# A change of phase in written order: the norms' rows, the next phase's first weight split, and four modulation blocks

## The chip, the cores and the metric

The kernel runs on one core of a Trainium2 chip. The metric is the device time of one execution in microseconds (us), lower is better. Below, TensorE (PE) multiplies, VectorE (DVE) and ScalarE (ACT) prepare operands, SyncE (SP) issues the DMAs.

## The reference, cut to what matters

One encoder layer over 256 tokens of 2048 channels, in fp32: half-step SwiGLU FFN, token mixing (a Conformer convolution on half of the channels beside differential attention), half-step SwiGLU FFN. Each part is normed before and after, and shifted, scaled and gated by a modulation vector.

```python
mod = silu(c) @ w_ada + b_ada                # 9 x 2048 values: sh, sc, gt of three parts
h = modulate(rms_norm(x, g_pre0), sh1, sc1)
x = x + 0.5 * gt1 * rms_norm(swiglu(h, w_gate, w_up, w_down), g_post0)
h = modulate(rms_norm(x, g_pre1), sh2, sc2)
u = h @ w_in                                 # convolution's two halves, q, k, v
m = concat(silu(layer_norm(depthwise(a * sigmoid(g)))), diff_attention(q, k, v)) @ w_out
x = x + gt2 * rms_norm(m, g_post1)
h = modulate(rms_norm(x, g_pre2), sh3, sc3)
x = x + 0.5 * gt3 * rms_norm(swiglu(h, ...), g_post2)
```

## The kernel before

**Weights.** Each fp32 product is made of three matmuls (L272 to L274) on operands split in a high and a low part. Weights come in blocks of 1 MB: `load` issues the DMA on SP into one of four `raw` buffers, ACT casts the high part (L160, tile `hi`, three buffers), DVE subtracts to get the low part (L162, `lo`); `parts` does all three. Activations are split in the same way by `split_act` (L173 on ACT, L175 on DVE). A raw buffer comes free when its `lo` is made. SP, ACT and DVE each take their instructions in the order that the program has them.

**Modulation.** `w_ada` comes in 144 blocks of 1 MB through the same four raw buffers. For each, DVE multiplies and sums (L183), and a tiny instruction (L189 or L192) adds bias or gain. A generator `bg` yields them one by one to the loops around.

**Phases.** The 256 tokens are two tiles of 128 rows. In order: FFN1 to 774 us; the first change of phase; the convolution's projection, attention, the output projection with the convolution's norm at 1057 to 1098 us; the second change; FFN2; the end. The last two column units of a projection run tile by tile in `m_last`, so that tile 0 is done first. What happens to a unit's sum is `evac` (add L486, sum of squares L236, gate L489; L847 in the mixing). After a tile's last unit, `close` norms the tile, adds it to x (L260) and `normed` makes the next phase's normed rows (L245 on ACT, L247 on DVE). A norm's small steps are L199, L204, L207 (square root on ACT, with a table load ahead of it) and L209. `front_of` then transposes the rows (L218), modulates them (L222, L225) and splits them (L227, L228), while the first weight blocks are multiplied (L311 to L313 after the first change, L272 to L274 after the second).

**What sets the order.** A scheduler orders the instructions of each engine from priorities, unless a stretch stands in `manual_schedule`, where the written order of the named engines holds. `issue_after` gives a stretch the place behind a named instruction.

**The convolution's norm.** `normalize` (L795 to L820) ends in four activation splits, `conv_acts`. The loop over the four column units behind it issues `MIXC` modulation blocks ahead of each unit's matmuls with the output weights `wo`, a list of 1 MB blocks, two for each unit and half.

## Time and profile before

| quantity | value |
|---|---|
| three runs | 1917.48, 1912.46, 1915.33 us; median 1915.33 |
| profiled execution | 1911.84 us, its span 1910.0 us |
| mean granted clock of TensorE | 0.984 |
| busy: PE, DVE, ACT | 1836.3, 1423.6, 821.4 us |

The span is the stretch from the first to the last recorded instruction; 1.84 us of the execution's own time lie around it. The profiled execution is the shortest of the four shown.

### The profile page before, as it was taken

How to read it: one execution, taken by the hardware profiler on the slowest of the kernel's cores; microseconds unless marked ns; L12 is line 12 of the kernel's file. 1: busy time of each engine (PE TensorE's matmuls, PEld its weight loads, DVE VectorE, ACT ScalarE, POOL GpSimd, SP SyncE). 2: the span in 40 equal slices, each digit the busy share in tenths (PEclk: the TensorE clock that was granted, in tenths of full speed). 3: DMA queues.
4: the chain of work that ended last, by engine and by line, in shares of the span. 5: the costliest groups of instructions: out<-in, count | busy, mean ns of one | idle time of the engine just before them, and what ended most of it. 6: DMA issues, size and time to landing. Idle time of an engine off the chain costs nothing.

```text
span 1910.0 us, 22064 instructions
## 1 busy us (share of the span) xinstructions
PE 1836.3 (96%) x8944; PEld 1542.5 (81%) x8944; DVE 1423.6 (75%) x1594; ACT 821.4 (43%) x852; POOL 6.0 (0%) x49
## 2 busy tenths in 40 slices
PE   5999999999999999799998897999999999999997
PEld 3788888888888888699997686788888888888886
DVE  7789999788889888688998967854555555555455
ACT  4544445433433334643554454544344333343342
POOL 0000000000000000000000000000000000000000
PEclk9999999999999999899999898999999999999999
DMA  9888877989999998355444665865665666565552
GB/s 362 320 317 330 337 278 290 358 345 361 357 357 370 349 367 323 122 182 185 157 174 157 242 241 202 331 238 205 236 220 205 235 220 226 215 235 210 194 193 72
DMA packets 68934, 492.58 MB, mean 258 GB/s; under 512 B 7648, under 2 KB 7776, under 8 KB 9440
## 3 DMA queue, kind: packets, MB, share of 16 engines
q1 hardware_dynamic: 68832, 491.17, 69.0%
q8 instruction: 70, 1.15, 0.2%
q14 instruction: 32, 0.26, 0.0%
HBM read 489.05 MB, written 2.10 MB: 257 GB/s over the span
## 4 chain that ended last, share of the span: by engine, by line
PE 89%; DVE 5%; ACT 3%; DMA 2%; issue 0%; SPq 0%; DVEq 0%; ACTq 0%
PE ps L273 29%; PE ps L274 29%; PE ps L272 28%; DVE lo L162 2%; DMA raw<-in_wgu 2%; ACT hi L160 1%; DVE raw L183 1%; PE ps L413 1%; ACT tmp L236 1%; PE ps L312 0%; PE ps L311 0%; DMA raw<-in_wk 0%; PE ps L313 0%; PE ps L678 0%; PE ps L218 0%
## 5 line engine op out<-in xcount | busy, mean ns | idle before, releaser
L162 DVE TENSOR_TENSOR lo<-raw,hi 128x2048 fp32r<-128x2048 f32 x314 | 718.5, 2290 | 359.8 <-ACT hi L160 359.1
L160 ACT CAST hi<-raw 128x2048 fp32r<-128x2048 f32 x314 | 600.3, 1912 | 732.4 <-PE ps L274 362.0
L272 PE MATMUL ps<-hi,big 128*128 128x512 f32 x2256 | 879.2, 395 | 16.9 <-ACT big L227 11.3
L273 PE MATMUL ps<-lo,big 128*128 128x512 f32 x2256 | 884.0, 392 | 2.8 <-DVE lo L162 2.8
L274 PE MATMUL ps<-hi,big 128*128 128x512 f32 x2256 | 881.5, 392 | 2.0 <-DVE big L175 1.2
L272 PEld LDWEIGHTS ps<-hi,big 128*128 128x128 f32 x2256 | 426.1, 189 | 106.4 <-ACT big L227 12.7
L273 PEld LDWEIGHTS ps<-lo,big 128*128 128x128 f32 x2256 | 426.5, 189 | 92.5 <-DVE lo L162 6.2
L274 PEld LDWEIGHTS ps<-hi,big 128*128 128x128 f32 x2256 | 425.7, 189 | 92.5 <-DVE big L175 2.5
L183 DVE SCALAR_TENSOR_TENSOR raw<-raw,crow 128x2048 f32<-128x2048 f32 x144 | 327.7, 2283 | 0.6 <-DMA raw<-in_wada 0.5
L272 PE MATMUL ps<-big,hi 128*128 128x256 f32 x448 | 127.3, 284 | 0.0
L273 PE MATMUL ps<-big,hi 128*128 128x256 f32 x448 | 126.7, 283 | 0.0
L274 PE MATMUL ps<-big,lo 128*128 128x256 f32 x448 | 126.7, 283 | 0.0
L630 DVE SCALAR_TENSOR_TENSOR big<-big,par,big 128x256 f32<-128x256 f32 x240 | 100.1, 477 | 0.0
L272 PEld LDWEIGHTS ps<-big,hi 128*128 128x128 f32 x448 | 85.9, 192 | 0.3 <-issue 0.3
L273 PEld LDWEIGHTS ps<-big,hi 128*128 128x128 f32 x448 | 86.0, 192 | 0.0
L274 PEld LDWEIGHTS ps<-big,lo 128*128 128x128 f32 x448 | 85.9, 192 | 0.0
L397 ACT ACTIVATE tmp<-ps 128x256 f32<-128x256 f32 x64 | 24.3, 384 | 96.3 <-PE ps L274 96.3
L486 DVE TENSOR_TENSOR big<-ps,big 128x512 f32<-128x512 f32 x48 | 32.9, 691 | 31.7 <-PE ps L274 31.7
L358 DVE TENSOR_TENSOR big<-ps,big 128x512 f32<-128x512 f32 x72 | 45.2, 681 | 5.4 <-PE ps L274 5.4
L398 DVE TENSOR_TENSOR tmp<-ps,tmp 128x256 f32<-128x256 f32 x64 | 26.1, 421 | 30.9 <-ACT tmp L397 30.9
L218 PE MATMUL ps<-ident,big 128*128 128x128 f32 x96 | 19.7, 297 | 29.6 <-DVE big L247 28.7
L173 ACT CAST big<-ps 128x512 fp32r<-128x512 f32 x44 | 25.8, 585 | 38.0 <-PE ps L413 38.0
(135 smaller groups left out, 742.6 us busy)
## 6 DMA issues: line engine op xcount, KB each, us to landing
raw<-in_wada SPq DMA_DIRECT2D x144, 1024.0 KB, 6.1
raw<-in_wgu SPq DMA_DIRECT2D x116, 1024.0 KB, 5.0
raw<-in_wd SPq DMA_DIRECT2D x88, 1024.0 KB, 5.0
raw<-in_wk SPq DMA_DIRECT2D x60, 1024.0 KB, 5.5
raw<-in_wqk SPq DMA_DIRECT2D x28, 1024.0 KB, 4.8
raw<-in_wo SPq DMA_DIRECT2D x16, 1024.0 KB, 4.8
raw<-in_wv SPq DMA_DIRECT2D x8, 1024.0 KB, 4.8
raw<-in_wkc SPq DMA_DIRECT2D x4, 1024.0 KB, 5.1
```

What stands on the lines that cost most here:

```text
L160: nc.scalar.copy(hi, raw)
L162: ins = nc.vector.tensor_tensor(out=lo, in0=raw, in1=hi.bitcast(F32), op=ALU.subtract)
L173: nc.scalar.copy(hi[:, :w], v[:, :w])
L183: nc.vector.scalar_tensor_tensor(out=raw, in0=raw, scalar=1.0, in1=crow, op0=ALU.mult, op1=ALU.mult, accum_out=acc)
L272: nc.tensor.matmul(o, ah, bh, start=first, stop=False)
L273: nc.tensor.matmul(o, ah, bl, start=False, stop=False)
L274: last_mm[0] = nc.tensor.matmul(o, al, bh, start=False, stop=last)
L358: nc.vector.tensor_tensor(out=a[t], in0=b[t], in1=a[t], op=ALU.add)
L397: nc.scalar.activation(v[:, o], b[t][:, :S], AF.Silu)
L398: nc.vector.tensor_tensor(out=v[:, o], in0=b[t][:, S:], in1=v[:, o], op=ALU.mult)
L486: nc.vector.tensor_tensor(out=y[t][u], in0=b, in1=y[t][u], op=ALU.add)
L630: nc.vector.scalar_tensor_tensor(out=cot(c), in0=vps[c][:, j:j + S], scalar=w, in1=cot(c), op0=ALU.mult, op1=ALU.add)
```

## The change

1. `evac` in the FFNs writes the gated sum to a new tile and no longer over the sum that ACT squares.
2. `m_last` takes `evac` and `close` apart from the matmuls: all matmuls of both tiles first, then, in written order for DVE and ACT, tile 0's `evac` and `close`, the first weight split of the next phase (`ahead`), tile 1's. A square root `warm` stands at its start.
3. The next phase's front is made earlier, so that its first split can be handed to `m_last`; `front_of` becomes `go_on`. A block that prepares the attention's constants moves ahead of FFN1.
4. `MIXC` goes from 2 to 4. Four modulation blocks go to the convolution's projection, one for each step; four stand behind the last activation split of the convolution's norm, where two per unit had stood.

```diff
-MIXC = 2
+MIXC = 4
@@ split_act
-        nc.vector.tensor_tensor(out=lo[:, :w], in0=v[:, :w], in1=hi[:, :w].bitcast(F32),
+        conv_last[0] = nc.vector.tensor_tensor(out=lo[:, :w], in0=v[:, :w], in1=hi[:, :w].bitcast(F32),
@@ Front and MFront (there: quarters)
+        def ahead(self):
+            self.first = parts(self.w[0])
...
-                self.wh, self.wl = parts(self.w[kt // per])
+                self.wh, self.wl = (kt == 0 and self.first) or parts(self.w[kt // per])
@@ m_last
+    ordered = lambda: tc.manual_schedule(engines={mybir.EngineType.DVE, mybir.EngineType.Activation})
+
-    def m_last(units, acts, after):
+    def m_last(units, acts, evac, close_, ahead):
...
-                after(u, t, banks[u][t])
+        with ordered():
+            if ahead:
+                nc.scalar.activation(small(1, "warm"), csil[:, 0:1], AF.Sqrt, scale=0.0)
+            xn = []
+            for t in range(NT):
+                for u, _, _ in units:
+                    evac(u, t, banks[u][t])
+                xn.append(close_(t))
+                if t == 0 and ahead:
+                    ahead()
+        return xn
@@ ffn, evac
-                    nc.vector.tensor_tensor(out=y[t][u], in0=y[t][u], in1=gb[u], op=ALU.mult)
-                if end and u == 3:
-                    xn.append(close(t, y, ss, 0.5, final))
+                    yg = big()
+                    nc.vector.tensor_tensor(out=yg, in0=y[t][u], in1=gb[u], op=ALU.mult)
+                    y[t][u] = yg
@@ convolution's projection
+        if 2 <= c < 2 + MIXC:
+            next(bg, None)
@@ output projection
-        for _ in range(MIXC):
-            next(bg, None)
+        if u == 0:
+            with tc.issue_after(conv_last[0].ins):
+                for _ in range(MIXC):
+                    next(bg, None)
```

The rows below are in the order in which an engine takes them; waits are not shown. In the changed kernel line numbers are shifted: cast L160 and low part L162 stay, activation split L173 and L175 become L175 and L177, modulation block L183, L189, L192 become L185, L191, L194, square sum L236 becomes L238, root L207 becomes L209, normed rows L245 and L247 become L247 and L249, add L486 becomes L510, gate L489 becomes L514, matmuls L272 to L274 become L274 to L276.

**First place: DVE, the last unit pair of FFN1.** The L486 and L489 (L510, L514) of `big_2524` and `big_2526` (`big_2540`, `big_2542`) are the adds and gates of unit 1; the splits read weights of units 2 and 3. Before:

```order
L183 SCALAR_TENSOR_TENSOR raw_5304,acc_5306<-raw_5304,crow 128x2048
L175 TENSOR_TENSOR big_5333<-raw_5329,big_5331 128x512
L189 TENSOR_TENSOR sh<-acc_5306,par 128x1
L175 TENSOR_TENSOR big_5337<-raw_5329,big_5335 128x512
L175 TENSOR_TENSOR big_5341<-raw_5329,big_5339 128x512
L175 TENSOR_TENSOR big_5345<-raw_5329,big_5343 128x512
L486 TENSOR_TENSOR big_2524<-ps_5237,big_2524 128x512
L486 TENSOR_TENSOR big_2526<-ps_5238,big_2526 128x512
L175 TENSOR_TENSOR big_5351<-raw_5347,big_5349 128x512
L489 TENSOR_TENSOR big_2524<-big_2524,ps_5232 128x512
L175 TENSOR_TENSOR big_5355<-raw_5347,big_5353 128x512
```

Changed:

```order
L510 TENSOR_TENSOR big_2540<-ps_5255,big_2540 128x512
L510 TENSOR_TENSOR big_2542<-ps_5256,big_2542 128x512
L514 TENSOR_TENSOR big_5330<-big_2540,ps_5250 128x512
L514 TENSOR_TENSOR big_5335<-big_2542,ps_5250 128x512
L177 TENSOR_TENSOR big_5353<-raw_5349,big_5351 128x512
L177 TENSOR_TENSOR big_5357<-raw_5349,big_5355 128x512
L162 TENSOR_TENSOR lo_5391<-raw_5387,hi_5389 128x2048
L177 TENSOR_TENSOR big_5361<-raw_5349,big_5359 128x512
L162 TENSOR_TENSOR lo_5397<-raw_5393,hi_5395 128x2048
```

The splits of the first block stood ahead of unit 1's adds and gates, and now stand behind all four of them.

**Second place: ACT, then DVE, between tile 0's norm and tile 1's.** `ssx` and `x_81` belong to tile 0, `ssy_439` to tile 1; the `hi` and `lo` are the next phase's weights `wkc`. ACT before:

```order
L236 ACTIVATE tmp_5447,ssx_984_5442<-x_81 128x512
L160 CAST hi_5691<-raw_5689 128x2048
L236 ACTIVATE tmp_5450,ssx_984_5442<-x_81 128x512
L236 ACTIVATE tmp_5453,ssx_984_5442<-x_81 128x512
L236 ACTIVATE tmp_5495,ssy_439_2231<-big_2637 128x512
L160 CAST hi_5777<-raw_5775 128x2048
L207 ACTIVATE sq_990_5458<-rs_989_5455 128x1
L236 ACTIVATE tmp_5523,ssy_439_2231<-big_2743 128x512
L245 ACTIVATE big_5464<-x_81,ri_991_5460 128x512
```

ACT changed (the table load ahead of the first root of this norm is still there, six rows higher; both `warm` roots stand at the program's start):

```order
L209 ACTIVATE sq_997_5532<-rs_996_5529 128x1
L247 ACTIVATE big_5538<-x_81,ri_998_5534 128x512
L247 ACTIVATE big_5542<-x_81,ri_998_5534 128x512
L160 CAST hi_5546<-raw_5544 128x2048
L160 CAST hi_5704<-raw_5702 128x2048
L160 CAST hi_5790<-raw_5788 128x2048
L238 ACTIVATE tmp_5551,ssy_439_2247<-big_2653 128x512
L238 ACTIVATE tmp_5556,ssy_439_2247<-big_2759 128x512
L209 ACTIVATE sq_1011_5563<-rs_1010_5560 128x1
```

DVE changed, from tile 0's normed rows:

```order
L249 TENSOR_SCALAR big_5540<-x_81,ri_998_5534 128x512
L162 TENSOR_TENSOR lo_5548<-raw_5544,hi_5546 128x2048
L510 TENSOR_TENSOR big_2653<-ps_5348,big_2653 128x512
L162 TENSOR_TENSOR lo_5706<-raw_5702,hi_5704 128x2048
L514 TENSOR_TENSOR big_5553<-big_2653,ps_5337 128x512
L510 TENSOR_TENSOR big_2759<-ps_5386,big_2759 128x512
L162 TENSOR_TENSOR lo_5792<-raw_5788,hi_5790 128x2048
L514 TENSOR_TENSOR big_5558<-big_2759,ps_5342 128x512
L201 TENSOR_REDUCE rs_1010_5560<-ssy_439_2247 128x1
L206 TENSOR_SCALAR rs_1010_5560<-rs_1010_5560 128x1
L211 RECIPROCAL ri_1012_5565<-sq_1011_5563 128x1
```

Two casts stood among tile 0's squares, the third ahead of them (not shown); now all three stand behind tile 0's normed rows and ahead of tile 1's square sums, and on DVE the three low parts stand between tile 1's adds and gates. Further on DVE a modulation block (`raw_6072`) now stands in the last norm of tile 1:

```order
L262 SCALAR_TENSOR_TENSOR x_82<-big_5558,ri_1012_5565,x_82 128x512
L201 TENSOR_REDUCE rs_1018_5580<-ssx_1013_5567 128x1
L206 TENSOR_SCALAR rs_1018_5580<-rs_1018_5580 128x1
L185 SCALAR_TENSOR_TENSOR raw_6072,acc_6074<-raw_6072,crow 128x2048
L211 RECIPROCAL ri_1020_5585<-sq_1019_5583 128x1
```

**Third place: SP, then DVE, at the convolution's norm.** SP before:

```order
L153 DMA raw_8688<-in_wada 128x2048
L153 DMA raw_8693<-in_wada 128x2048
L153 DMA raw_8698<-in_wo 128x2048
L153 DMA raw_8728<-in_wo 128x2048
L153 DMA raw_8773<-in_wada 128x2048
L153 DMA raw_8778<-in_wada 128x2048
L153 DMA raw_8783<-in_wo 128x2048
L153 DMA raw_8813<-in_wo 128x2048
L153 DMA raw_8858<-in_wada 128x2048
L153 DMA raw_8863<-in_wada 128x2048
```

SP changed:

```order
L153 DMA raw_8604<-in_wo 128x2048
L153 DMA raw_8634<-in_wo 128x2048
L153 DMA raw_8721<-in_wada 128x2048
L153 DMA raw_8726<-in_wada 128x2048
L153 DMA raw_8731<-in_wada 128x2048
L153 DMA raw_8736<-in_wada 128x2048
L153 DMA raw_8741<-in_wo 128x2048
L153 DMA raw_8771<-in_wo 128x2048
L153 DMA raw_8816<-in_wo 128x2048
L153 DMA raw_8846<-in_wo 128x2048
```

DVE changed, from the last activation splits to the first `wo` splits:

```order
L177 TENSOR_TENSOR big_8672<-big_5937,big_8670 128x512
L177 TENSOR_TENSOR big_8680<-big_5938,big_8678 128x512
L177 TENSOR_TENSOR big_8688<-big_5939,big_8686 128x512
L185 SCALAR_TENSOR_TENSOR raw_8721,acc_8723<-raw_8721,crow 128x2048
L185 SCALAR_TENSOR_TENSOR raw_8726,acc_8728<-raw_8726,crow 128x2048
L194 SCALAR_TENSOR_TENSOR gs<-acc_8723,par 128x1
L191 TENSOR_TENSOR sh<-acc_8728,par 128x1
L185 SCALAR_TENSOR_TENSOR raw_8731,acc_8733<-raw_8731,crow 128x2048
L185 SCALAR_TENSOR_TENSOR raw_8736,acc_8738<-raw_8736,crow 128x2048
L194 SCALAR_TENSOR_TENSOR gs<-acc_8733,par 128x1
L191 TENSOR_TENSOR sh<-acc_8738,par 128x1
L162 TENSOR_TENSOR lo_8745<-raw_8741,hi_8743 128x2048
L162 TENSOR_TENSOR lo_8775<-raw_8771,hi_8773 128x2048
```

The blocks of `wada` went in pairs between pairs of `wo`. Now four go in a row, and the next `wo` take the buffers that these four leave.

## Rows read from the trace of the kernel before

**Rows 1.** The page, part 1: busy us, share, instructions of each engine.

```profile
PE 1836.3 (96%) x8944; PEld 1542.5 (81%) x8944; DVE 1423.6 (75%) x1594; ACT 821.4 (43%) x852; POOL 6.0 (0%) x49
```

**Rows 2.** Waits of TensorE by what released it: total us, times, longest.

```profile
PE ps L218 <- DVE big L247: 28.7, 5, 10.9
```

**Rows 3.** TensorE, first change: start, us, line, tiles, idle before, releaser.

```profile
751.98 0.47 PE L272 MATMUL ps<-big,big 128*128 128x512 f32 x1
...
780.44 0.90 PE L218 MATMUL ps<-ident,big 128*128 128x128 f32 x3 [6.35 <-DVE big L247]
...
788.14 0.79 PE L311 MATMUL ps<-big,hi 128*128 128x256 f32 x2 [0.79 <-ACT big L227]
```

**Rows 4.** VectorE from the last unit pair of FFN1 to the second tile's norm.

```profile
750.71 1.37 DVE L486 TENSOR_TENSOR big<-ps,big 128x512 f32<-128x512 f32 x2 [0.80 <-PE ps L274]
...
776.33 0.68 DVE L486 TENSOR_TENSOR big<-ps,big 128x512 f32<-128x512 f32 x1
777.03 2.29 DVE L162 TENSOR_TENSOR lo<-raw,hi 128x2048 fp32r<-128x2048 f32 x1
...
781.50 2.74 DVE L260 SCALAR_TENSOR_TENSOR x<-big,ri,x 128x512 f32<-128x512 f32 x4
...
785.90 0.88 DVE L247 TENSOR_SCALAR big<-x,ri 128x512 f32<-128x512 f32 x2
```

**Rows 5.** ScalarE at the first change.

```profile
752.58 0.62 ACT L236 ACTIVATE tmp<-big 128x512 f32<-128x512 f32 x1
...
765.68 1.28 ACT L207 ACT_TABLE_LOAD   x1
766.98 0.20 ACT L207 ACTIVATE sq<-rs 128x1 f32<-128x1 f32 x1
...
775.12 1.88 ACT L160 CAST hi<-raw 128x2048 fp32r<-128x2048 f32 x1
```

**Rows 6.** VectorE at the convolution's norm.

```profile
1084.27 1.74 DVE L813 RECIPROCAL tmp<-tmp 128x256 f32<-128x256 f32 x1
...
1088.35 3.25 DVE L818 SCALAR_TENSOR_TENSOR big<-big,par,tmp 128x256 f32<-128x256 f32 x8
1091.52 2.28 DVE L183 SCALAR_TENSOR_TENSOR raw<-raw,crow 128x2048 f32<-128x2048 f32 x1
...
1097.35 1.28 DVE L175 TENSOR_TENSOR big<-big,big 128x512 fp32r<-128x512 f32 x2
```

**Rows 7.** TensorE at the convolution's norm.

```profile
1079.62 0.67 PE L783 MATMUL ps<-tmp,onesc 128*128 128x256 f32 x2
...
1086.65 0.65 PE L131 MATMUL ps<-ident,gt 128*128 128x128 f32 x4 [1.60 <-ACT tmp L853]
1090.73 0.80 PE L272 MATMUL ps<-hi,big 128*128 128x512 f32 x1 [3.43 <-ACT big L173]
...
1094.47 1.22 PE L274 MATMUL ps<-hi,big 128*128 128x512 f32 x2 [1.24 <-DVE big L175]
```

**Rows 8.** Busy time by stretch; the column behind POOL is TensorE's granted clock.

```profile
830.00:860.00 30.00, 30.00 (x252) 30.00 (x252) 27.89 (x46) 11.62 (x9) 0.00 (x0) 1.00 0.59 213
1088.00:1098.00 10.00, 6.03 (x13) 4.31 (x14) 10.00 (x19) 5.37 (x12) 0.00 (x0) 0.50 0.66 235
```

**Rows 9.** DMA issues between 1040 and 1172 us: KB each, median us to landing.

```profile
raw<-in_wo SPq DMA_DIRECT2D x10, 1024.0 KB, 4.9
```

**Rows 10.** VectorE at the second change.

```profile
1149.44 2.29 DVE L162 TENSOR_TENSOR lo<-raw,hi 128x2048 fp32r<-128x2048 f32 x1 [1.73 <-ACT hi L160]
1151.65 0.68 DVE L847 TENSOR_TENSOR big<-ps,tmp 128x512 f32<-128x512 f32 x1
...
1158.47 2.29 DVE L162 TENSOR_TENSOR lo<-raw,hi 128x2048 fp32r<-128x2048 f32 x1 [1.53 <-ACT hi L160]
...
1160.87 0.88 DVE L247 TENSOR_SCALAR big<-x,ri 128x512 f32<-128x512 f32 x2
```

**Rows 11.** VectorE at the end of the program.

```profile
1901.92 0.69 DVE L489 TENSOR_TENSOR big<-big,ps 128x512 f32<-128x512 f32 x1 [1.13 <-ACT tmp L236]
```

More of the change, by code (lines that the diff above doesn't have):

```diff
@@ L168, in parts @@
         return hi, lo
+    conv_last = [None]
     def split_act(v, w=512):
@@ L296, in __init__ @@
             self.sum = None
+            self.first = None
+        def ahead(self):
+            self.first = parts(self.w[0])
         def step(self, kt, first, last):
@@ L335, in __init__, with ahead @@
             self.sum = None
+            self.first = None
+        def ahead(self):
+            self.first = quarters(self.w[0])
         def step(self, kt, first, last):
@@ L343, in step @@
                 if i % 4 == 0:
-                    self.parts = quarters(self.w[i // 4])
+                    self.parts = (i == 0 and self.first) or quarters(self.w[i // 4])
                 for t in range(NT):
@@ L451, in leave, with ffn @@
             left.append(f)
-    def ffn(l, h, front, facts, wgu, wd, bg, every, final):
+    def ffn(l, h, front, facts, wgu, wd, bg, every, ahead):
         y = [[None] * 4 for _ in range(NT)]
@@ L462, in tick @@
                 next(bg, None)
-        xn = []
         hacts = [(a[:, :S], a[:, S:]) for a in h]
@@ L502, in ffn @@
                     gb[u] = gate_row(l, u)
-                m_last([(u, srcs(u), None) for u in range(4 - N_LAST, 4)], acts, evac)
+                xn = m_last([(u, srcs(u), None) for u in range(4 - N_LAST, 4)], acts, evac,
+                            lambda t: close(t, y, ss, 0.5, not ahead), ahead)
         return xn
@@ L556, in first_front, with go_on @@
         return h, facts
-    def front_of(l, xn, wk, late):
-        h = []
-        front = Front(wk, h, SET[l]) if l == 1 else MFront(wk, h, SET[l] // 2)
+    def go_on(l, xn, h, front, late):
         n_late = 0
@@ L571, in front_of @@
                 front.step(i - LEAD, i == LEAD, i == NK + LEAD - 1)
-        return h, front
     xn = []
@@ L590, in block_kernel @@
     h, facts = first_front(xn, wk1, ada_of([(m, kt) for kt in range(NK) for m in (1, 0)]), bg)
-    xn = ffn(0, h, None, facts, wgu1, wd1, bg, EVERY1, False)
     lv = cp.tile([P, 4, DH], F32, tag="lv", name="lv")
@@ L612, in block_kernel @@
     nc.vector.tensor_scalar(out=nlam, in0=nlam, scalar1=-LAM_INIT, scalar2=None, op0=ALU.add)
-    h = []
+    h1 = []
+    front = Front(wkc[0], h1, SET[1])
+    xn = ffn(0, h, None, facts, wgu1, wd1, bg, EVERY1, front.ahead)
+    h = h1
     need([(m, kt) for m in (3, 4) for kt in range(NK)], bg)
-    h, front = front_of(1, xn, wkc[0], iter(()))
+    go_on(1, xn, h, front, iter(()))
     co = [big() for _ in range(NC_ // 2)]
@@ L840, in block_kernel @@
     need([(5, kt) for kt in range(NK)], bg)
-    xn = []
     gb = {}
@@ L847, in mix_evac @@
         nc.vector.tensor_tensor(out=y[t][u], in0=b, in1=gb[u], op=ALU.mult)
-        if u == 3:
-            xn.append(close(t, y, ss, 1.0, False))
     for u in range(4):
@@ L861, in block_kernel @@
                 mix_evac(u, t, open_[u][t])
-    m_last([(u, of_conv(u), open_[u]) for u in range(4 - N_LAST, 4)], conv_acts, mix_evac)
-    h, front = front_of(2, xn, wk2[0], bg)
-    ffn(2, h, front, {}, wgu2, wd2, ada_of([(8, kt) for kt in range(NK)]), 6, True)
+    h = []
+    front = MFront(wk2[0], h, SET[2] // 2)
+    xn = m_last([(u, of_conv(u), open_[u]) for u in range(4 - N_LAST, 4)], conv_acts, mix_evac,
+                lambda t: close(t, y, ss, 1.0, False), front.ahead)
+    go_on(2, xn, h, front, bg)
+    ffn(2, h, front, {}, wgu2, wd2, ada_of([(8, kt) for kt in range(NK)]), 6, None)
 def _layout(i):
```

## The prediction, made before the changed kernel was run

> **What bounds the kernel now.** I read the page first: TensorE is busy for 1836.3 of 1910.0 us, 96% [rows 1], so an edit is worth what it adds to or takes from TensorE's waits, and VectorE at 75% matters where it stands ahead of TensorE. The list of TensorE's waits comes next: the largest is the transposes L218 behind the normed rows L247, 28.7 us in five waits, the longest 10.9 [rows 2]; these are the two changes of phase and the start. The timelines then show each place. At the first change the matmuls end at 780.44 - 6.35 = 774.09, and the next phase's first matmul starts at 788.14 [rows 3], 14.05 us later. At the convolution's norm TensorE waits 1.60, 3.43 and 1.24 us, 6.27 in all, from 1085.05 on [rows 7], with the clock at half (0.50) from 1088 to 1098 [rows 8]. In the second change the last normed rows start at 1160.87 [rows 10].
>
> **The change, part by part, made against the profiled execution's 1911.84 us.** I follow the printed order of the changed kernel, with durations from the rows.
>
> *First change, the splits ahead of it.* In the changed order the casts and low parts of units 2 and 3 stand behind unit 1's adds, squares and gates. The second square of unit 1 now has no cast ahead of it, so it ends near 752.9 instead of 752.58 + 0.62 + 0.19 = 753.4 [rows 5], but the first cast (0.6) only then starts: 753.5. The matmul that started at 751.98 [rows 3] starts at 753.5, 1.5 us late; behind it TensorE waits some 0.4 for the first low part and some 0.6 for the first full cast of 1.9. 96 matmuls took 751.98 to 774.09, 0.23 each; they now end near 776.4, **+2.3**. Fifty-six of them, the last one of tile 0 among these, are done at 753.5 + 1.0 + 56 x 0.23 = 767.4.
>
> *First change, the norms.* Tile 0: add 0.7, square 0.8, table load 1.28 [rows 5], root and reciprocal 0.5, so L260 starts at 770.7; an undisturbed L260 to L247 takes 785.90 - 781.50 = 4.40 [rows 4], so the normed rows start at 775.1. ACT gives its two rows until 776.4 and then takes the three weight casts, 1.9 each [rows 5], to 782.1. VectorE has the three low parts, 2.2 us from one start to the next instruction's (2.29 with the end that overlaps) [rows 4], between tile 1's adds and gates: the first at 778.3, after the cast, then add, low part, gate, add, low part, gate, each small one 0.6. That ends at 778.3 + 3 x 2.2 + 4 x 0.6 = 787.3. What is queued there is tile 1's whole norm, and TensorE waits for that. Sum, root and reciprocal 0.8, then 4.40: 792.5. In this last norm stands a modulation block ahead of the reciprocal. Its buffer comes free with the third low part at 786.7, a block lands 4.9 us after its issue [rows 9], 791.6, and it holds VectorE for 2.2 from 791.9 on: the normed rows start at 794.4. From there to the first matmul it was 788.14 - 785.90 = 2.24 [rows 3, 4]: 796.6. That is 8.5 late, **2.3 + 6.2**. Before, one low part lay beside TensorE's own matmuls and one of them, 777.03, in the way. The bounds: 785.3 if nothing stood between (776.4 + 0.7 + 0.8 + 0.8 + 4.40 + 2.24), that is -2.8, and with a second block's wait +11.
>
> A rule says otherwise about the table load: the Trainium skill, ScalarE: Activation LUTs, section What ACT_TABLE_LOAD costs, counts 1.28 us and a drain of 1.38 for each switch of set. The row shows the load at 765.68 and the root at 766.98, 1.30 later [rows 5], with no drain; by the page tile 0's rows and all behind them would come 1.4 later and the whole sum would be 16.2 instead of 14.8. The measurement decides here.
>
> *`warm`.* Both roots stand at the program's start, so no load leaves a norm's path; 0, between -1.28 and 0 per change if they stood where they are written.
>
> *Convolution's norm.* The matmuls of the second mean (1079.62 [rows 7]) stand nine matmuls earlier, 2.1 us; with root and reciprocal (1.74 [rows 6]) the products L818, at 1088.35 before, start near 1081.2, because the modulation blocks and low parts between are gone. The last activation split, done at 1097.35 + 1.28 = 1098.6 [rows 6], is done near 1087.9 (I take ACT's part, 6.7 us behind the first product). This is 10 us early, and not what TensorE waits for next. The four modulation blocks sit in all four raw buffers, and the first `wo` block can be issued only when the first of them is through VectorE, behind the norm: 1087.9 + 2.2 = 1090.1; it lands 4.9 later [rows 9], 1095.0, is cast until 1096.9, and its low part stands behind all four blocks and their tiny sums: 1087.9 + 4 x 2.2 + 0.6 = 1097.3, plus 2.2 = 1099.5. TensorE has two matmuls without the low part (0.85 at half clock) and the gate's (0.65): from 1085.05 to 1099.5 it waits 14.45 - 1.5 = 12.95 instead of 6.27. The half clock lies in both: before it covered thirteen matmuls [rows 8], now about as many behind the resume. **+6.7**; bounds +2.5 (first block landed sooner and the low part ahead of the last two modulation blocks) and +9.
>
> *The four blocks in the projection.* 4 x 2.28 us of VectorE where TensorE is full and VectorE busy 27.89 of 30 us [rows 8]. 0: the convolution's own products are fillers that can slip; without that cover up to 9.
>
> *Second change.* Before, a low part stood ahead of tile 1's gate (1149.44 to 1151.65) and one in its last norm (1158.47) [rows 10]. Now one stands ahead of the gates and one behind the first sum, waiting for its cast; the last norm is free. I get the normed rows at 1160.2, and one split of the next phase less made beforehand, which VectorE catches up. **-1**, between -4 (nothing between) and +2.2 (the missing split lies in the way).
>
> *End.* The same lateness of the splits costs 1.2; the last gate, which waited 1.13 for the square [rows 11], no longer does, and then the square is what ends last: 0.6 back. **+0.6**. The constants' block ahead of FFN1 lies beside VectorE's free quarter: 0.
>
> Sum: 2.3 + 6.2 + 6.7 - 1.0 + 0.6 = **+14.8**, 1926.6 for the profiled execution's like. That one is the shortest of four; the mean of 1911.84, 1912.46, 1915.33 and 1917.48 is 1914.3, so I forecast 1914.3 + 14.8 = **1929**.
>
> **Rivals.** *The norm alone sets the resume.* If at all three places the weights' splits are ready whenever a norm ends, the first change gives -2.8, the norm of the convolution -6.27 and the 2.6 that thirteen matmuls lose at half clock, the second -4, the end +0.6: -15, 1899. For it: the norm's rows do become contiguous. Against: three casts stand by the printed order ahead of tile 1's first square, and the `wo` blocks have no buffer. It decides at whether tile 0's rows are done before about 768, so that three casts and low parts fit ahead of 776.4; I have 775.1.
>
> *The buffers are not in the way.* If the modulation blocks pass VectorE ahead of the norm's end, so that `wo` has landed by 1088, the convolution's norm gives -8.9 and the rest stays: 8.5 - 8.9 - 1.0 + 0.6 = -0.8, 1914, no change. Against: the printed order has all four behind the last activation split.
>
> *The blocks in the projection are not covered*: up to +9, 1938.
>
> **How the numbers follow.** The forecast has 0.70, the buffers' rival 0.14, the norm alone 0.12, the uncovered blocks 0.04. No change means within 0.3%, 5.7 us, of the median 1915.33, about what three runs can tell. The forecast's own range is 1921 to 1938 (first change 11 to 4, convolution 9 to 2.5, second change 2.2 to -4, not all at one end). To hold 8 in 10 the range reaches down to the buffers' rival: 1913 to 1938. Faster 0.12, same 0.14, slower 0.74.
>
> **What would show it.** Right: the first L311's like starts 20 us behind the last matmul of FFN1 instead of 14; on ACT three casts of 1.9 in a row ahead of tile 1's square; a VectorE low part ends the wait at the convolution's norm, near 13 us in all, with `wo` landing behind the first modulation block. Wrong: normed rows of tile 1 within 9 us of TensorE's last matmul, `wo` issued ahead of the modulation blocks, or waits in the projection, where there were none.

## The result, and the profile after

The changed kernel takes 1926.96 us (median of 1925.57 to 1927.87), the kernel before 1914.76 beside it (1912.46 to 1917.48): ratio 1.007, 95% interval 1.0054 to 1.0085. It is slower, as forecast; 1929 was 2 us too high.

The profiled execution took 1927.59 us with a span of 1925.8. The first part of its page, and TensorE's waits by what released them (total us, times, longest):

```profile
PE 1836.6 (95%) x8944; PEld 1542.2 (80%) x8944; DVE 1424.6 (74%) x1594; ACT 822.7 (43%) x855; POOL 6.0 (0%) x49
```

```profile
PE ps L220 <- DVE big L249: 34.9, 4, 18.1
PE ps L274 <- ACT hi L160: 13.5, 4, 9.3
...
PE ps L274 <- ACT big L175: 2.3, 2, 1.2
```

TensorE is busy as long as before [rows 1] to 0.3 us, so nearly the whole difference is idle time. The wait for the normed rows (L220 behind L249, which were L218 and L247) grew from 28.7 us [rows 2] to 34.9, and the list has 13.5 us of waiting for a weight's cast (L274 behind L160), the longest 9.3. The timeline shows where. TensorE in the changed kernel:

```profile
754.46 0.50 PE L274 MATMUL ps<-big,big 128*128 128x512 f32 x1 [1.17 <-ACT big L175]
...
777.20 0.40 PE L276 MATMUL ps<-hi,big 128*128 128x512 f32 x1
...
796.04 0.90 PE L220 MATMUL ps<-ident,big 128*128 128x128 f32 x3 [18.12 <-DVE big L249]
797.74 0.80 PE L317 MATMUL ps<-big,hi 128*128 128x256 f32 x2 [0.80 <-ACT big L229]
...
1060.41 0.90 PE L788 MATMUL ps<-ident,tmp 128*128 128x128 f32 x3 [5.85 <-DVE tmp L778]
...
1096.56 0.81 PE L131 MATMUL ps<-ident,gt 128*128 128x128 f32 x4 [2.34 <-ACT tmp L878]
1106.69 1.22 PE L274 MATMUL ps<-hi,big 128*128 128x512 f32 x2 [9.31 <-ACT hi L160]
1109.26 0.80 PE L275 MATMUL ps<-lo,big 128*128 128x512 f32 x1 [1.36 <-DVE lo L162]
...
1176.54 0.90 PE L220 MATMUL ps<-ident,big 128*128 128x128 f32 x3 [10.01 <-DVE big L249]
1178.23 0.80 PE L274 MATMUL ps<-hi,big 128*128 128x512 f32 x1 [0.80 <-ACT big L229]
```

The kernel before, at the rows of these places that were not shown yet (TensorE, then VectorE):

```profile
1051.05 1.33 PE L760 MATMUL ps<-ident,tmp 128*128 128x128 f32 x5 [5.85 <-DVE tmp L750]
...
1161.41 0.90 PE L218 MATMUL ps<-ident,big 128*128 128x128 f32 x3 [10.90 <-DVE big L247]
1163.11 0.80 PE L272 MATMUL ps<-hi,big 128*128 128x512 f32 x1 [0.80 <-ACT big L227]
```

```profile
764.15 0.69 DVE L486 TENSOR_TENSOR big<-ps,big 128x512 f32<-128x512 f32 x1 [0.52 <-PE ps L274]
```

VectorE in the changed kernel, at the first change, at the convolution's norm and at the second change:

```profile
751.77 1.37 DVE L510 TENSOR_TENSOR big<-ps,big 128x512 f32<-128x512 f32 x2 [3.09 <-PE ps L276]
...
768.55 0.69 DVE L510 TENSOR_TENSOR big<-ps,big 128x512 f32<-128x512 f32 x1 [0.86 <-PE ps L276]
...
779.37 2.29 DVE L162 TENSOR_TENSOR lo<-raw,hi 128x2048 fp32r<-128x2048 f32 x1 [2.28 <-ACT hi L160]
...
785.58 2.28 DVE L162 TENSOR_TENSOR lo<-raw,hi 128x2048 fp32r<-128x2048 f32 x1
...
788.38 0.15 DVE L201 TENSOR_REDUCE rs<-ssy 128x1 f32<-128x4 f32 x1
...
793.04 2.28 DVE L185 SCALAR_TENSOR_TENSOR raw<-raw,crow 128x2048 f32<-128x2048 f32 x1
...
795.50 0.88 DVE L249 TENSOR_SCALAR big<-x,ri 128x512 f32<-128x512 f32 x2
...
1090.66 3.25 DVE L846 SCALAR_TENSOR_TENSOR big<-big,par,tmp 128x256 f32<-128x256 f32 x8
...
1097.06 0.69 DVE L177 TENSOR_TENSOR big<-big,big 128x512 fp32r<-128x512 f32 x1 [0.71 <-ACT big L175]
1097.67 2.28 DVE L185 SCALAR_TENSOR_TENSOR raw<-raw,crow 128x2048 f32<-128x2048 f32 x1
...
1104.51 2.28 DVE L185 SCALAR_TENSOR_TENSOR raw<-raw,crow 128x2048 f32<-128x2048 f32 x1
...
1106.92 2.29 DVE L162 TENSOR_TENSOR lo<-raw,hi 128x2048 fp32r<-128x2048 f32 x1
...
1165.37 2.29 DVE L162 TENSOR_TENSOR lo<-raw,hi 128x2048 fp32r<-128x2048 f32 x1 [2.28 <-ACT hi L160]
...
1168.85 2.28 DVE L162 TENSOR_TENSOR lo<-raw,hi 128x2048 fp32r<-128x2048 f32 x1
...
1176.00 0.88 DVE L249 TENSOR_SCALAR big<-x,ri 128x512 f32<-128x512 f32 x2
```

ScalarE at the first change and at the convolution's norm, and SyncE's DMA issues there:

```profile
770.08 1.28 ACT L209 ACT_TABLE_LOAD   x1
771.38 0.20 ACT L209 ACTIVATE sq<-rs 128x1 f32<-128x1 f32 x1
...
777.46 5.48 ACT L160 CAST hi<-raw 128x2048 fp32r<-128x2048 f32 x3
...
1104.73 1.90 ACT L160 CAST hi<-raw 128x2048 fp32r<-128x2048 f32 x1 [7.71 <-DMA raw<-in_wo]
```

```profile
1051.82 28.01 SPq L153 DMA_DIRECT2D raw<-in_wada  x4
1099.99 9.57 SPq L153 DMA_DIRECT2D raw<-in_wo  x5
```

Read these from top to bottom at one place. At the first change three casts in a row hold ScalarE for 5.48 us; the low parts follow on VectorE among tile 1's adds and gates; tile 1's norm begins only at 788.38, and a modulation row of 2.28 us (L185) stands in it. At the convolution's norm the last activation split (L177) is over at 1097.75, but the first `wo` block is issued at 1099.99, when the first L185 has given its buffer back, and ScalarE waits 7.71 us for it. Its cast ends at 1106.63; the fourth block's row and the tiny sums behind it end at 1106.92, and only then comes the low part. So the transfer and the rows ahead of the low part end within 0.3 us of each other.

The two profiled executions, stretch by stretch, cut at rows that both have:

| stretch | before | after | difference | predicted |
|---|---|---|---|---|
| start to unit 1's first add (L486, now L510) | 750.71 | 751.77 | +1.06 | 0 |
| to the projection's first matmul (L311, L317) | 788.14 | 797.74 | +8.54 | +8.5 |
| to the transposes L760, L788 | 1051.05 | 1060.41 | -0.24 | 0 |
| to the last matmul of the mixing (1161.41 - 10.90, 1176.54 - 10.01) | 1150.51 | 1166.53 | +6.66 | +6.7 |
| to FFN2's first matmul (L272, L274) | 1163.11 | 1178.23 | -0.90 | -1.0 |
| to the end of the span | 1910.0 | 1925.8 | +0.7 | +0.6 |

The differences add up to 15.8, the difference of the spans.

### The profile page after: what moved, and what is told of

Read it like the earlier page. It is cut to its first block, busy times and chain, and to the rows that moved or that the text cites. A ratio compares the mean times of both kernels' runs of the same rounds, so it can differ in the third digit from the quotient of the medians.

```text
span 1925.8 us, 22069 instructions
## 1 busy us (share of the span) xinstructions
PE 1836.6 (95%) x8944; PEld 1542.2 (80%) x8944; DVE 1424.6 (74%) x1594; ACT 822.7 (43%) x855; POOL 6.0 (0%) x49
## 4 chain that ended last, share of the span: by engine, by line
PE 90%; DVE 4%; ACT 3%; DMA 2%; issue 1%; SPq 0%; DVEq 0%; ACTq 0%
PE ps L275 29%; PE ps L276 29%; PE ps L274 29%; DVE lo L162 2%; DVE raw L185 1%; ACT hi L160 1%; DMA raw<-in_wgu 1%; PE ps L423 1%; ACT tmp L238 1%; DMA x<-in_x 0%; PE ps L318 0%; PE ps L317 0%; PE ps L319 0%; PE ps L706 0%; DMA raw<-in_wk 0%
## 5 line engine op out<-in xcount | busy, mean ns | idle before, releaser
L162 DVE TENSOR_TENSOR lo<-raw,hi 128x2048 fp32r<-128x2048 f32 x314 | 718.5, 2290 | 371.1 <-ACT hi L160 370.8
L160 ACT CAST hi<-raw 128x2048 fp32r<-128x2048 f32 x314 | 600.0, 1912 | 731.0 <-PE ps L276 357.4
L274 PE MATMUL ps<-hi,big 128*128 128x512 f32 x2256 | 875.2, 395 | 24.7 <-ACT hi L160 13.5
L276 PE MATMUL ps<-hi,big 128*128 128x512 f32 x2256 | 881.1, 391 | 0.3 <-DVE big L230 0.3
L274 PEld LDWEIGHTS ps<-hi,big 128*128 128x128 f32 x2256 | 425.8, 189 | 114.2 <-ACT hi L160 15.0
L276 PEld LDWEIGHTS ps<-hi,big 128*128 128x128 f32 x2256 | 425.7, 189 | 90.3 <-DVE big L230 1.0
L185 DVE SCALAR_TENSOR_TENSOR raw<-raw,crow 128x2048 f32<-128x2048 f32 x144 | 327.6, 2284 | 0.2
L274 PE MATMUL ps<-big,hi 128*128 128x256 f32 x448 | 127.3, 284 | 0.0
L276 PE MATMUL ps<-big,lo 128*128 128x256 f32 x448 | 126.7, 283 | 0.0
L274 PEld LDWEIGHTS ps<-big,hi 128*128 128x128 f32 x448 | 85.9, 192 | 0.3 <-issue 0.3
L276 PEld LDWEIGHTS ps<-big,lo 128*128 128x128 f32 x448 | 85.9, 192 | 0.0
L510 DVE TENSOR_TENSOR big<-ps,big 128x512 f32<-128x512 f32 x48 | 32.8, 690 | 29.1 <-PE ps L276 29.1
L220 PE MATMUL ps<-ident,big 128*128 128x128 f32 x96 | 18.9, 290 | 35.9 <-DVE big L249 34.9
L220 PEld LDWEIGHTS ps<-ident,big 128*128 128x128 f32 x96 | 12.9, 147 | 40.8 <-DVE big L249 36.1
```

The costliest lines, as they stand in the source:

```text
L160: nc.scalar.copy(hi, raw)
L162: ins = nc.vector.tensor_tensor(out=lo, in0=raw, in1=hi.bitcast(F32), op=ALU.subtract)
L185: nc.vector.scalar_tensor_tensor(out=raw, in0=raw, scalar=1.0, in1=crow, op0=ALU.mult, op1=ALU.mult, accum_out=acc)
L220: nc.tensor.transpose(b[:, t * P:(t + 1) * P], src[:, o:o + P], ident)
L274: nc.tensor.matmul(o, ah, bh, start=first, stop=False)
L276: last_mm[0] = nc.tensor.matmul(o, al, bh, start=False, stop=last)
```

## The experiments

The table gives every kernel's median, the 95% interval of its ratio to the kernel before on the same chip (whose medians there were 1913.5 for the first four, 1914.28 for the next four and 1914.65 for the last three), and three stretches of its profile, cut as above: **A** from unit 1's first add to the projection's first matmul (before: 788.14 - 750.71 = 37.43), **B** from the transposes L760 or L788 to the mixing's last matmul (1150.51 - 1051.05 = 99.46), **C** from there to FFN2's first matmul (1163.11 - 1150.51 = 12.60).

| kernel | us | ratio, its 95% interval | A | B | C |
|---|---|---|---|---|---|
| before | 1914.76 | 1 | 37.43 | 99.46 | 12.60 |
| changed | 1926.96 | 1.0054 to 1.0085 | 45.97 | 106.12 | 11.70 |
| mix_as_before | 1918.52 | 1.0008 to 1.0032 | 43.97 | 99.58 | 11.71 |
| mix_alone | 1923.08 | 1.0029 to 1.0062 | 38.82 | 106.17 | 12.78 |
| mix_all_in_projection | 1920.52 | 1.0020 to 1.0044 | 47.96 | 96.34 | 11.97 |
| split_behind | 1921.11 | 1.0019 to 1.0045 | 36.76 | 106.11 | 10.02 |
| splits_first | 1921.37 | 1.0026 to 1.0054 | 42.56 | 105.09 | 11.72 |
| blocks_behind_front | 1925.49 | 1.0048 to 1.0075 | 44.02 | 105.70 | 11.71 |
| two_at_norm | 1915.64 | 0.9999 to 1.0019 | 44.03 | 95.79 | 11.90 |
| combo_proj | 1904.83 | 0.9939 to 0.9967 | 33.59 | 95.26 | 9.72 |
| constants_back | 1927.18 | 1.0051 to 1.0077 | 45.94 | 105.71 | 11.94 |
| combo_first_only | 1904.18 | 0.9934 to 0.9959 | 33.58 | 94.96 | 11.68 |
| combo_mix_before | 1908.20 | 0.9951 to 0.9978 | 33.58 | 99.04 | 9.74 |

My theory was the sum of the prediction: the order at the first change and the buffers at the convolution's norm each cost some 7 to 8 us. The rivals were that only one of the two does, or that the modulation blocks cost their VectorE time and not the buffers.

### The modulation blocks undone, and alone

The changed kernel with the blocks as before:

```diff
-MIXC = 4
+MIXC = 2
-        if 2 <= c < 2 + MIXC:
-            next(bg, None)
...
-        if u == 0:
-            with tc.issue_after(conv_last[0].ins):
-                for _ in range(MIXC):
-                    next(bg, None)
+        for _ in range(MIXC):
+            next(bg, None)
```

> The changed kernel with its modulation blocks back where the kernel before has them (two ahead of each column unit's wo matmuls, none in the projection); the written order of the norms and the first split stay. My theory: the convolution's norm loses the 6.7 us that the blocks' hold on the raw buffers costs there (TensorE's waits go from 13.0 back to about 6.3 us), and tile 1's norm at the first change loses the 2.2 us of the block that stands in it: 1927 - 8.9 = 1918. Rival, that the written order of the norms costs all of it and the blocks nothing: 1927.

Then the kernel before with this one part of the change (the diff the other way round, and `conv_last` set in `split_act`):

> The kernel before with the modulation blocks' part of the change alone. My theory: +6.7 at the convolution's norm, and one block of 2.2 now also stands in tile 1's norm at the first change, waiting for its landing, about +2: 1914.8 + 8.7 = 1923.5, with wo landing only after the first of the four blocks. Rival, that the blocks' place costs only together with the written order: 1915.

Measured: 1918.52, +5.0 against its batch's 1913.5, and 1923.08, +9.6. The two halves add up to 14.6, beside 12.2 for the whole. Stretch B is 99.58 without the blocks' move and 106.17 with it alone, so all of the loss at the convolution's norm comes from the blocks. A falls by 2.0 when they go back: the L185 in tile 1's norm is theirs.

### All eight blocks in the projection

```diff
-        if 2 <= c < 2 + MIXC:
+        if c < 2 * MIXC:
             next(bg, None)
...
-        if u == 0:
-            with tc.issue_after(conv_last[0].ins):
-                for _ in range(MIXC):
-                    next(bg, None)
```

> The changed kernel with all eight modulation blocks in the convolution's projection, one for each step, and none at the convolution's norm. My theory: wo has landed and is split when the activations come, so TensorE's 13.0 us of waits there shrink to 1 or less and the half clock goes with them (about 2.5), and no block stands in tile 1's norm (2.2): 1927 - 16 = 1911 or so. Rival, that VectorE has no room for four more blocks of 2.2 in the projection, where it is busiest: 8.8 come back as waits there, 1920.

1920.52: the time is the rival's, the reason isn't. The projection had room (1062.87 - 800.85 = 262.0 us, against 262.7 in the changed kernel). B did fall, by 9.8, but A rose by 2.0, and the time fell by 6.4 in place of the 16 that 1911 would have taken. VectorE at this kernel's first change shows why:

```profile
789.46 0.15 DVE L201 TENSOR_REDUCE rs<-ssy 128x1 f32<-128x4 f32 x1
789.53 2.28 DVE L185 SCALAR_TENSOR_TENSOR raw<-raw,crow 128x2048 f32<-128x2048 f32 x1
...
791.74 0.15 DVE L206 TENSOR_SCALAR rs<-rs 128x1 f32<-128x1 f32 x1
791.80 2.28 DVE L185 SCALAR_TENSOR_TENSOR raw<-raw,crow 128x2048 f32<-128x2048 f32 x1
```

Two modulation rows of the projection's first steps stand between steps of tile 1's norm that take 0.15 us each, where one had stood. At the other end the `wo` low parts, which now come early, stand among the rows of the convolution's norm, so it ends later than I had counted: a wait of 4.24 us is left there, where I had put 1 or less. The next section shows the same wait in another kernel, with its rows.

### The projection's blocks held behind the first splits, and two left at the norm

`behind_dve` gives a block's VectorE row its place behind the last normed or modulated row that VectorE was given.

```diff
         if 2 <= c < 2 + MIXC:
-            next(bg, None)
+            behind_dve(next, bg, None)
```

> The changed kernel with the four modulation blocks that it put into the projection written so that their VectorE row may not stand ahead of the second layer's first weight splits: no L185 is left in tile 1's last norm. My theory (that L185 costs its whole 2.2 to 2.3 us there, because the norm's rows follow one another on VectorE): the L220 wait falls from 18.1 to about 15.9, the time to about 1924.5. Rival (the row stands in a gap of the chain between two norm steps): the wait and the time stay, 1926.5 to 1927.

L220's wait fell from 18.1 to 16.2, A by 1.95, the time by 1.5. The times alone can't tell the two kernels apart, since their intervals overlap; but A is 43.97 to 44.03 in the three kernels without that row whose order is otherwise the changed one (mix_as_before, this one, two_at_norm), and 45.94 and 45.97 in the two that have it. The row costs nearly its whole length there. The second kernel has six such blocks and two behind the norm:

```diff
-        if 2 <= c < 2 + MIXC:
-            next(bg, None)
+        if 2 <= c:
+            behind_dve(next, bg, None)
...
-                for _ in range(MIXC):
+                for _ in range(MIXC // 2):
                     next(bg, None)
```

> As blocks_behind_front, but six modulation blocks go in the projection and two, in place of four, behind the convolution's norm. My theory (four blocks hold all four raw buffers, so wo's first lands only after the first of their VectorE rows): with two of the buffers left to wo, its first casts no longer wait for a transfer of their own; TensorE's waits about the convolution's norm fall from 13.0 to some 4 to 6.5 us, and the time to about 1916 to 1918. Rival (the blocks cost their VectorE time there, 2.2 us each): 13.0 falls by 4.4 to 8.6, the time to about 1920; a cast that waits for wo's transfer stays. Third: wo's low parts, which now come sooner, stand among the norm's rows and take as much again, as they did with all eight in the projection: waits at about 10, time about 1922.

1915.64, 11.3 below the changed kernel, 9.85 below its twin with four blocks at the norm. TensorE, VectorE, ScalarE and SyncE's issues at the convolution's norm of this kernel:

```profile
1096.79 0.50 PE L274 MATMUL ps<-hi,big 128*128 128x512 f32 x1 [4.24 <-ACT big L175]
```

```profile
1090.93 3.26 DVE L846 SCALAR_TENSOR_TENSOR big<-big,par,tmp 128x256 f32<-128x256 f32 x8
1094.10 2.29 DVE L162 TENSOR_TENSOR lo<-raw,hi 128x2048 fp32r<-128x2048 f32 x1
1096.77 0.69 DVE L177 TENSOR_TENSOR big<-big,big 128x512 fp32r<-128x512 f32 x1 [0.38 <-ACT big L175]
...
1101.42 2.28 DVE L185 SCALAR_TENSOR_TENSOR raw<-raw,crow 128x2048 f32<-128x2048 f32 x1
```

```profile
1091.71 1.90 ACT L160 CAST hi<-raw 128x2048 fp32r<-128x2048 f32 x1 [4.32 <-PE ps L276]
1093.63 1.28 ACT L848 ACT_TABLE_LOAD   x1
1094.92 1.31 ACT L848 ACTIVATE big<-big,par 128x256 f32<-128x256 f32 x3
```

```profile
1050.23 7.35 SPq L153 DMA_DIRECT2D raw<-in_wada  x2
1072.45 31.61 SPq L153 DMA_DIRECT2D raw<-in_wo  x6
```

With two of the four buffers left to it, `wo` is issued from 1072.45 on. TensorE waits 4.24 us instead of 13.0, and now for the norm's own split (L175), no longer for a `wo` block. Two rows of 2.28 less explain 4.6 of that fall of 8.8 at most; here the two that are left start at 1101.42, when TensorE has already gone on. So the buffers were what was short; a kernel with all four rows at the norm and buffers to spare was not run, and two_at_norm takes off two rows as well.

The third possibility is there too, at a lower price: three `wo` low parts stand among the norm's rows (1081.47, 1086.94, 1094.10). The last of them is not what TensorE waits for, since VectorE then still waits 0.38 us for ScalarE. On ScalarE a `wo` cast stands ahead of the table load of the norm's last activations (L848), which therefore start 3.99 us behind the first product (1090.93, 1094.92); in the changed kernel, without that cast, it was 0.52 (1090.66, 1091.18). So the 4.24 us that are left follow again from a row of the next weights, now a cast that came early. What it is worth to move that cast was not tried.

### The two halves of the order at the first change

The first split of the next phase behind tile 1's norm, at both changes:

```diff
-                if t == 0 and ahead:
+                if t == NT - 1 and ahead:
```

> The changed kernel with the next phase's first split written behind tile 1's norm instead of between the tiles; nothing else differs. My theory: at the first change no cast stands ahead of tile 1's squares and no low part between its adds and gates, so its normed rows start some 7 us behind TensorE's last matmul instead of 18.6, and the first weight's cast and low part, 1.9 and 2.2, now come behind them and cost about 3 of the 9 or so gained there: -6 to -8. At the second change the one split that stands in the way goes, and comes back behind the norm: between -1 and +2. In all 1927 - 6 = 1921. Rival, that the splits between the tiles are hidden and the norm's own chain is what is long: no change or slower, 1927 to 1931.

The splits of units 2 and 3 ahead of unit 1's adds again (`m_prep` is the part of `m_last` that makes them):

```diff
                 banks = m_unit(srcs(u), acts, tick=tick)
+                if end and u == 3 - N_LAST:
+                    prep = m_prep([(v, srcs(v), None) for v in range(4 - N_LAST, 4)])
                 for t in range(NT):
                     evac(u, t, banks[t])
```

> The changed kernel with one thing undone: the weight splits of the pair of units 2 and 3 are written ahead of unit 1's adds again (the first split between the tiles, the constants' block and the modulation blocks stay as changed). My theory (VectorE and ScalarE reach the end of the pair late, because its splits stand behind unit 1's adds, squares and gates): 2.3 us come back at the first change of phase (18.1 to about 15.8 us of wait ahead of L220) and about 0.6 to 1.2 us at the end of the last layer, so about 1923.5 beside 1926.5 to 1927 for the changed kernel. Rival (that stretch is set by the norm and the casts alone, the place of the splits is hidden): no change, 1926.5 or more, with the L220 wait still at 18.

split_behind took 9.2 off A, to 36.76, and 1.7 off C, yet the time fell by 5.8 only. Its profile starts 1.4 us later (753.17 us against 751.77), and from FFN2's first matmul to the end it takes 3.7 us longer (1919.3 - 1168.08 = 751.2 against 1925.8 - 1178.23 = 747.6). The 60 us behind FFN2's first matmul, in split_behind and then in the changed kernel (the first column behind the sum is TensorE's busy time with its matmuls, the one behind POOL the granted clock):

```profile
1168.10:1228.10 60.00, 57.64 (x249) 46.25 (x250) 53.83 (x63) 24.92 (x30) 0.00 (x0) 0.95 0.85 324
```

```profile
1178.20:1238.20 60.00, 59.26 (x262) 48.08 (x263) 52.78 (x63) 26.08 (x31) 0.00 (x0) 0.97 0.81 310
```

13 matmuls fewer are done, 3.0 us at 0.23 each. 1.6 of them are idle time, in which TensorE waits 2.0 us for casts and low parts of weights instead of 0.3; the granted clock is lower too, 0.95 against 0.97. So FFN2's first split made early pays there. After the first change it does not: the projection takes 262.0 us in split_behind and 262.7 in the changed kernel.

splits_first took 3.4 off A, and the wait of 1.17 us ahead of the last pair (754.46 above) went. The 3.4 did not come where I had put it: L220's wait fell to 17.22 only, not to 15.8, and TensorE reaches that wait 2.5 us sooner, counted from unit 1's first add. Tile 0's last add, on which its norm hangs, starts 13.37 us behind that first add (752.16, 765.53) instead of 16.78 (751.77, 768.55).

The time is 5.6 us less by the medians, more than the 2.9 to 3.5 that I had expected. The 3.4 of A and the same wait of 1.17 at the end of the program, which goes too (the list of the changed kernel has two such waits, L274 behind L175), make 4.6. The rest is not explained. By the profiles B is 1.0 shorter and the projection 1.2 (261.5 us against 262.7), and the latter goes with TensorE's clock. TensorE in the 7 us behind the resume of the projection, in the changed kernel, in splits_first and in constants_back (the next section), whose order there is the changed kernel's:

```profile
797.70:804.70 7.00, 6.96 (x37) 6.96 (x38) 2.07 (x5) 1.83 (x5) 0.00 (x0) 0.59 0.25 107
```

```profile
794.70:801.70 7.00, 6.98 (x47) 6.98 (x48) 2.49 (x6) 2.34 (x6) 0.00 (x0) 0.78 0.24 101
```

```profile
798.30:805.30 7.00, 6.97 (x41) 6.98 (x42) 2.39 (x6) 1.97 (x5) 0.00 (x0) 0.67 0.26 109
```

The granted clock is at its lower level for longer in the changed kernel than in splits_first, 0.59 against 0.78 on the mean, and ten matmuls are missing. But constants_back has 0.67 behind a wait of 18.11 us, as long as the changed kernel's 18.12, and the kernel before 0.56 and 35 matmuls behind 5.11 and 0.79 us. So the clock behind the resume differs between profiles also where the order is the same, and it is not shown that the splits' place sets it.

### The constants' block

The block is written behind FFN1 again, `h1`, `front` and the call of `ffn` ahead of it; nothing else differs from the changed kernel.

```diff
+    h1 = []
+    front = Front(wkc[0], h1, SET[1])
+    xn = ffn(0, h, None, facts, wgu1, wd1, bg, EVERY1, front.ahead)
...
-    h1 = []
-    front = Front(wkc[0], h1, SET[1])
-    xn = ffn(0, h, None, facts, wgu1, wd1, bg, EVERY1, front.ahead)
```

> The changed kernel with one thing undone: the constants' block is written behind the first layer again. My theory (it is hidden; the 1.2 us wait ahead of the last pair of the first layer comes from the late splits, since it went with splits_first): the wait at about 753 us stays 1.17 and the time stays at 1925 to 1927. Rival (the block's instructions hold the start or that pair up): the last pair begins 1 us sooner, 1925 to 1926 at most.

1927.18, no change, and the 1.17 us are still there. The block is hidden where it was moved.

### The parts that pay, together

combo_proj has the diffs of splits_first and split_behind, the constants back, and all eight blocks in the projection through `behind_dve`. combo_mix_before is the same with the blocks as in the kernel before.

> All the parts undone or moved that the earlier runs priced: the pair's splits first (-2.3 and -0.6 to -1.2), the first split of the next phase behind tile 1's norm (-6, the low parts no longer ahead of the norm), the constants' block back behind the first layer's front (0 to -1), and all eight modulation blocks in the projection behind the second layer's first splits (-9.8 at the convolution's norm less 0, and no L185 in tile 1's norm, -2.2). If these add, about 1926.5 - 2.3 - 0.6 - 6 - 9.8 - 2.2 = 1905.6, below both kernels by 8 or more. Rival (the gains overlap, since each is the last of several waits that end nearly together): 1911 to 1914, no better than before.

> combo_proj with the modulation blocks as in the kernel before (two in each of the convolution's units). By the traces the stretch from the convolution's norm to the second change takes 95.3 us in combo_proj and 99.5 to 99.6 with the blocks as before, so my theory gives 4.2 us more than combo_proj, about 1909; the order of splits and norms alone is then worth 5 us against the kernel before. Rival (the gain of combo_proj comes from the blocks alone): 1913 to 1915.

And combo_proj with the early split kept at the second change (`prep` is set at the first alone):

```diff
-                if t == NT - 1 and ahead:
+                if t == (NT - 1 if prep else 0) and ahead:
```

> combo_proj with the first split of the next phase behind tile 1's norm at the first change of phase alone, and between the tiles, as in the changed kernel, at the second. By the traces of combo_proj and of the changed kernel the second change takes 9.7 us in the one and 11.7 in the other, but the 54 us that follow take 3.0 more in the first (the splits behind the first one come late, 1.05 us and many smaller waits), so my theory gives 1.0 us less than combo_proj, about 1903.8. Rival (what stands early delays the norm there as it does at the first change): 2 us more, about 1907.

1904.83, 1908.20 and 1904.18 in the order of the three expectations: all three beat both kernels, combo_proj by 9.5 us against the kernel before. The gains add nearly as priced (1905.6 and 1909 expected). combo_mix_before shows that order alone is worth 6.5 us, and that the blocks' place gives 3.4 more. The choice at the second change can't be told from the times, 0.65 us apart: combo_first_only is 2.0 slower in C and gets that back behind it. TensorE's waits in combo_first_only, the fastest:

```profile
PE ps L220 <- DVE big L249: 24.4, 4, 10.0
...
PE ps L274 <- ACT big L175: 4.2, 1, 4.2
```

The longest wait of 18.1 us is gone; the wait for a `wo` cast at the convolution's norm too, and 4.2 us of waiting for the norm's own split are left there, as in two_at_norm.

## Why the prediction was right

**What bounds.** Right: busy time is unchanged to 0.3 us, and the difference is idle time in the places that were named. The first sign came too: the projection starts 797.74 - (777.20 + 0.40) = 20.1 us behind FFN1's last matmul, where the prediction had 20.

**First change, +8.5 predicted, +8.54 measured.** Taking off the 1.06 by which everything starts later, the casts end at 777.46 + 5.48 - 1.06 = 781.9 (782.1 predicted), the sum behind the last low part and gate starts at 788.38 - 1.06 = 787.3 (787.3), the normed rows at 795.50 - 1.06 = 794.4 (794.4), the first matmul at 796.7 (796.6). The modulation row stands in the last norm. TensorE's last matmul (L276 at 777.20) ends at 777.20 + 0.40 - 1.06 = 776.5 (776.4), so the 2.3 for late splits is right for TensorE; three transposes of tile 0 follow it before the wait of 18.12 begins. On the way that ended last, which leads over tile 0's norm, late splits cost more: tile 0's last add starts at 768.55 - 1.06 = 767.5, where the prediction has tile 0's last matmul done at 767.4, and that is 3.3 behind the kernel before (764.15). The splits put first give 3.4 in splits_first and 3.2 between split_behind and combo_proj (36.76 - 33.59). So the times of the prediction hold, but about 1 us of its second term, 6.2, belongs to the late splits: 5.1 to 5.4 are left for the early split and the row behind it. The changed kernel's A stands 12.4 above the uninterrupted 33.59 of combo_proj, 3.2 for late splits and 9.2 for the early split with its row (some 2 of them the row, by blocks_behind_front); the kernel before stands 3.8 above it, for the low part [rows 4] and what else lay between its norms.

**Table load.** The Trainium skill, ScalarE: Activation LUTs, section What ACT_TABLE_LOAD costs, counts a drain of 1.38 us beside the load's 1.28. The load stands at 770.08 and the root at 771.38, 1.30 later, as in [rows 5]: no drain. That the spans differ by 15.8, nearer the page's sum of 16.2, is the later start and not a drain.

**Convolution's norm, +6.7 predicted, +6.66 measured**, and by the steps named. The stage starts 9.36 later than before; less that, the first product stands at 1081.3 (1081.2 predicted), the last activation split is done at 1088.4 (1087.9), the first block's row at 1090.5 (1090.1), the first `wo` block is cast from 1095.4 (1095.0), the low part is done at 1099.9 (1099.5). The waits are 13.01 us (12.95). That the sum agrees to 0.04 is luck in part: B lies between 105.09 and 106.17 in the six kernels that have the same four blocks there. two_at_norm shows that the buffers are the cause, within the limit named there. In my expectation for all eight blocks in the projection the step that failed is another: I had counted the freed blocks as gone from the path, while the scheduler set two into tile 1's norm at the first change, and the early `wo` splits into the convolution's.

**Second change, -1 predicted, -0.90 measured; end, +0.6 and +0.7.** The two low parts stand where the prediction put them (1165.37 ahead of the gates, 1168.85 behind the first sum), and the normed rows at 1176.00 are 16.02 of lateness behind 1159.98 (1160.2 predicted). Late splits cost 1.17 at the end, the gate that no longer waits gives some back.

**The blocks in the projection and the constants, 0 each.** Right: -0.24, and no change in constants_back.

**The size.** +14.8 on the mean of four runs gave 1929, 2 above the median. The profiled spans differ by 15.8, the medians by 12.2. The profile of before was the fastest of its runs (1911.84 to 1917.48), and the profile of after is near the slowest of its own (1927.59 of 1925.57 to 1927.87), and 1.06 of the 15.8 lies ahead of unit 1's first add. That add stands between 749.63 and 754.43 us in the thirteen profiles. The two kernels with the old first layer are the lowest (749.63, 750.71), but combo_first_only and combo_proj, which are alike up to there, have 751.00 and 754.30, and the constants' block isn't it (752.39 without its move). So whether 1 us of the start belongs to the change stays open.

**Rivals.** The norm alone sets the resume: not so, the weights ended the wait at the convolution's norm, and low parts stood ahead of tile 1's at both changes; combo_proj, where tile 1's norms are free of such rows at both changes while three `wo` low parts and a cast still stand in the convolution's norm, comes nearest to it, 1904.8 where 1899 was put. Buffers not in the way: wrong in the changed kernel; two_at_norm is nearest to that case, 1915.64 where 1914 was put. Uncovered blocks: wrong, the projection takes 262.7 us with the four blocks and 262.9 before.

## What to carry to other kernels

Work that is written "between" two latency chains is paid if it waits for a transfer or a cast of its own: here 9.2 us at the first change, with a row of 2.28 that a scheduler slipped in. Look at every row that stands between two short steps of the chain that is waited for, on VectorE and on ScalarE. A side stream that shares a ring of buffers with the next phase's weights can cost more by the buffers that it holds than by its own time: leave the next phase as many as it needs to start. The same early split was a loss where the next weights were not short and nearly even where they were, so price each place by itself.

## What the runs showed of the hardware

A wait can cost more than its length, and its length does not tell how much more. In the changed kernel the granted clock was at its lower level (1.2 GHz) for most of the 7 us behind the wait of 18.12 us, 0.59 on the mean, and 37 matmuls were done; those on the 128x256 operands followed each other every 0.21 us up to 803.3 us and every 0.12 us from 803.8 on. Behind 18.11 us in constants_back the mean was 0.67, with 41 matmuls; behind 17.22 us in splits_first 0.78 and 47; behind 7.00 us and 2.03 in combo_first_only 0.71 and 44; behind 5.11 us and 0.79 in the kernel before 0.56 and 35.

The start of a program varies: unit 1's first add stands at 751.00 and 754.30 us in combo_first_only and combo_proj, which are alike up to there, and at 751.21 to 754.43 us in six kernels with the changed first layer that differ only behind it. What sets it was not tried.
